# A two-block transformer kernel on one core: the mixer starts with its gated columns, and softmax sums are divided out by products with a diagonal matrix

## The chip, the cores and the metric

The kernel runs on one core of a Trainium2 chip. The metric is device microseconds for one execution. Five queues of instructions matter: PE (TensorE, matrix products; PEld is its weight load), DVE (VectorE), ACT (ScalarE), POOL (GpSimd) and SP, which issues every DMA. Each takes its instructions strictly in the order in which they were written out when the program was built; they wait for each other by semaphores.

## The reference, cut to what matters

The program is a chain of two blocks. The first has two layers, each a mixer, a cross-attention and a gated feed-forward part; the second is a single layer with a recurrent mixer and sixteen experts. Only the mixer of the first block's two layers is touched. It reads 512 tokens of width 1024:

```
proj = x @ w_in + b_in
c_q, c_kv, k_r, u = split(proj)          # 256, 256, 32 and 2 * 512 columns
q  = rms_norm(c_q) @ w_uq                # 8 heads of 64 + 32 columns
kv = rms_norm(c_kv) @ w_ukv              # keys and values of 8 heads
p  = softmax(mask(q @ k.T) * scale)      # by blocks of 128 queries, causal
y_att  = p @ v
a, g = split(u); h = a * sigmoid(g)      # the gated half
y_conv = silu(layer_norm(conv31(h)))     # 31 taps along the tokens
out = concat(y_att, y_conv) @ w_o
```

## The kernel before

Most products are made of three: each float32 operand is split into a rounded high part and a low rest (`fp32r`), and `mm3` (lines 157 to 159) sums high by high, high by low and low by high. `weight` loads a weight (`wr`), rounds it on ACT (`wh`, line 148) and subtracts on DVE or, for every n-th weight, on POOL (`wl`, line 152); `pool_lo` is that n. The few matrices of plain float32 go through `nc.tensor.matmul` directly. `tr` (line 163) transposes 128 by 128 values on PE with the constant `ident`.

The mixer's parts, in the order of the code before: `latent(0)` makes and normalises the query latent, token block by token block (its DVE lines are 463, 183, 469 and 130, its POOL line 185 is the reciprocal root); `queries` projects it to heads and rotates (DVE lines 261 to 266); `gated(0)` makes two of the four 128-column chunks of h (the product with the whole 512 tokens as moving side, then ACT line 487 and DVE line 488); `latent(1)` makes the key and value latent; `gated(2)` makes the other two chunks. Then come key and value weights (line 542), values, and eight heads.

For each head and each of its four query blocks, a score product (line 601, 128 to 512 columns, float32) is reduced to its maximum on DVE (line 603), exponentiated on ACT with the sum on the side (line 606), the sum is inverted on DVE (line 608), the block is scaled by that on ACT (line 609), transposed on PE (line 163) and copied out by DVE (line 613) for the product with the values (line 622). In the code the convolution comes after the heads: chunks 0 and 2 are 31 DVE instructions each (666, 670, copy 671), chunks 1 and 3 are products with one tap on ACT (677) or POOL (679) and a sum on POOL (680), through two buffers `cm`. 

The code's order is not the order of the engines: a scheduler writes each engine's list when the program is built, and fills it with whatever it holds to be ready, earlier code first. So convolution taps are strewn among the other instructions. Line numbers below are those of the code before; in the code after, lines from 103 on stand 3 higher, those from the heads' loop 3 to 5 higher.

Of the kernel before, what the change touches and what calls it, by code (L numbers as in the profile page):

```python
# [10 lines left out]
F32 = mybir.dt.float32  # L11
F32R = mybir.dt.float32r
I32 = mybir.dt.int32
AF = mybir.ActivationFunctionType
# [42 lines left out]
class Builder:  # L57
# [42 lines left out]

    def sm(self, shape=(1,), dt=F32):
        return self.sp.tile([128] + list(shape), dt, name="sm", tag="sm", bufs=20)

    def ring(self, *ids):

        state = [0]

        def bank():
            i = ids[state[0] % len(ids)]
            state[0] += 1  # L110
            return self.pp.tile([128, 512], F32, name=f"q{i}", tag=f"q{i}", bufs=1)

        return bank
# [324 lines left out]
    def mixer(self, l, xT):  # L438
        nc, A = self.nc, self.A
# [15 lines left out]
        def latent(c):  # L455
            c0, n = (0, 256) if c == 0 else (256, 288)
            ring = self.ring(0, 1, 2, 3)
            ps = self.tok_cols(w_in, c0, n, xT, ring, tokens_first=c == 0)
            ss = self.sm([NT])
            ct = [self.s2([2, 256]) for _ in range(2)]  # L460
            for t in range(NT):
                x = ct[t // 2][:, t % 2, :]
                nc.vector.tensor_tensor(out=x, in0=ps[t][:, 0:256], in1=bc[:, c0:c0 + 256], op=OP.add)
                if c == 1:
                    nc.vector.tensor_tensor(out=krt[:, t, 64:96], in0=ps[t][:, 256:288], in1=bk, op=OP.add)
                junk = self.s2([256])
                nc.scalar.activation(junk, x, AF.Square, accum_out=ss[:, t:t + 1])
                r = self.rstd(ss[:, t:t + 1], 1.0 / 256, EPS)
                nc.vector.scalar_tensor_tensor(x, x, r, gn[:, c, :], op0=OP.mult, op1=OP.mult)
                pt = ring()[:, :256].rearrange("p (k t) -> p k t", k=2)  # L470
                for k in range(2):
                    self.tr(pt[:, k, :], x[:, k * 128:(k + 1) * 128])
                dst = (cq, ck)[c]
                s = slice(t * 128, (t + 1) * 128)
                self.split_ps(pt, dst[:, 0, :, s], dst[:, 1, :, s])
# [19 lines left out]
        def queries():  # L495

            ring = self.ring(4, 5, 6)
            for i in range(2):
                nc.scalar.activation(qt[i][:, :, :, 96:100],
                                     self.qm[:, 2 * i:2 * i + 2, None, :].to_broadcast([128, 2, 8, 4]), AF.Copy)  # L500
            for hf in range(2):
                wh, wl = self.weight(A["mla_w_uq"][l][:, hf * 384:(hf + 1) * 384]
                                     .rearrange("(k p) f -> p k f", p=128), [2, 384])
                for t in range(NT):
                    ps = ring()[:, :384]
                    s = slice(t * 128, (t + 1) * 128)
                    for k in range(2):
                        self.mm3(ps, cq[:, 0, k, s], cq[:, 1, k, s], wh[:, k, :], wl[:, k, :], k == 0, k == 1)
                    nc.scalar.activation(qt[t // 2][:, t % 2, 4 * hf:4 * hf + 4, 0:96],
                                         ps.rearrange("p (h d) -> p h d", h=4), AF.Copy, scale=QSCALE)  # L510
            for i in range(2):
                self.rope(qt[i][:, :, :, 64:80], qt[i][:, :, :, 80:96], 2 * i, 2, 8)

        latent(0)
        queries()
        gated(0)
        latent(1)
        gated(2)
        self.pool_lo = 5
        kr = krt.rearrange("p t (h d) -> p t h d", h=1)  # L520
        self.rope(kr[:, :, :, 64:80], kr[:, :, :, 80:96], 0, NT, 1)

# [35 lines left out]
        mm = nc.tensor.matmul  # L558
# [31 lines left out]
        for h in range(HEADS):  # L590
            if h + 1 < HEADS:
                if h % 2 == 1:
                    keys(h + 1)
                query(h + 1)
            kh, q = key(h), qs.pop(h)
            pair = h // 2 % 2
            pts = [(ptas[pair][i], ptbs[pair][:, i]) for i in range(2)]
            for t in range(NT):
                nv = (t + 1) * 128
                ps = sring()  # L600
                mm(ps[:, :nv], q[:100, t * 128:nv], kh[:100, :nv], start=True, stop=True)
                nm = self.sm([1])
                nc.vector.tensor_reduce(nm, ps[:, :nv], axis=AX.X, op=OP.max, negate=True)
                p = self.s2([512])
                sum_ = self.sm([1])
                nc.scalar.activation(p[:, :nv], ps[:, :nv], AF.Exp, bias=nm, accum_out=sum_)
                rc = self.sm([1])
                nc.vector.reciprocal(rc, sum_)
                nc.scalar.activation(p[:, :nv], p[:, :nv], AF.Copy, scale=rc)
                pt = tring().rearrange("p (k t) -> p k t", k=4)  # L610
                for k in range(t + 1):
                    self.tr(pt[:, k, :], p[:, k * 128:(k + 1) * 128])
                nc.vector.tensor_copy(pts[h % 2][t // 2][:, :t + 1, (t % 2) * 128:(t % 2) * 128 + 128], pt[:, :t + 1, :])
            if h % 2:

                ps = cring()
                for i in range(2):
                    n = 2 * i + 2
                    for k in range(n):
                        for j in range(2):  # L620
                            hd = slice((h - 1 + j) * 64, (h + j) * 64)
                            mm(ps[j * 64:j * 64 + 64, i * 256:(i + 1) * 256], vt[:, k, hd], pts[j][i][:, k, :],  # L622
                               start=k == 0, stop=k == n - 1)
                self.split_ps(ps, yT.hi(h // 2), yT.lo(h // 2))
# [218 lines left out]

    def first_block(self):
        A = self.A
        self.phase(t8=11, s2=10, cm=2)
        self.rope_tables()
        xT = self.transposed(self.ring(4, 5, 6, 7))
        for l in range(LAYERS):
            yT = self.mixer(l, xT)  # L850
            self.stage(f"cln{l}")
            gb = self.ln_params(A["ln1_g"][l], A["ln1_b"][l])
            self.out_proj(A["mix_w_o"][l], yT, gb)
            self.stage(f"wo{l}")
            mT, kT = self.memory_keys(l)
            xT = self.transposed(self.ring(4, 5, 6, 7))
            vh, vl = self.memory_values(l, mT)
            self.stage(f"kv{l}")
            self.dump(f"ln1_{l}", self.xt)
            self.stage(f"ln1_{l}")  # L860
            oT = self.cross(l, xT, kT, vh, vl)
            self.stage(f"cross{l}")
            gb2 = self.ln_params(A["ln2_g"][l], A["ln2_b"][l])
            if l + 1 == LAYERS and "ctx_2" in A:
                self.setup2()
            xT, ring = FM(self, 8, 512), self.ring(3, 4)
            self.out_proj(A["xa_w_o"][l], oT, gb2, lambda t: self.tr_tile(self.xt[:, t, :], xT, t, ring=ring))
            self.dump(f"ln2_{l}", self.xt)
            self.stage(f"ln2_{l}")
            self.side = (self.adaln, self.context)[l]() if "ctx_2" in A else None  # L870

            def norm3():
                gb3 = self.ln_params(A["ln3_g"][l], A["ln3_b"][l])
                token = self.token_start() if l + 1 == LAYERS and "ctx_2" in A else lambda t: None

                def finish(t):
                    self.layer_norm(t, gb3)
                    token(t)

                return finish  # L880

            self.ffn(l, xT, norm3, iter(self.TICKS[l] * 64))
            self.dump(f"ln3_{l}", self.xt)
            self.stage(f"ln3_{l}")
            if l + 1 < LAYERS:
                xT = self.transposed(self.ring(4, 5, 6, 7))
# [944 lines left out]
    def second_block(self):  # L1831
        if self.dbg and self.dbg.get("skip1"):
            self.setup2()
            self.phase(t8=11, s2=10, cm=2)
            self.pc = self.ring(3, 7)
            for part in (self.adaln, self.context):
                for _ in part():
                    pass
            self.stage("ctx")
            token = self.token_start()  # L1840
            for t in range(NT):
                token(t)
        cat = self.token_mixer()
        self.stage("cat")
        self.moe(cat)
        self.phase()
# [58 lines left out]
```

## Time and profile before

| what | value |
|---|---|
| median of 3 runs | 2583.95 us (2583.64 to 2584.36) |
| the profiled execution | 2585.66 us, its span 2583.9 us |
| PE busy | 2436.6 us, 94% of the span |
| DVE busy | 1334.9 us, 52% |
| ACT busy | 899.2 us, 35% |
| POOL busy | 624.7 us, 24% |
| mixer of layer 0 up to its first softmax | 0 to 123.1 us |
| its heads | 123.1 to 184.5 us and a little more |
| mixer of layer 1: first softmax, last | 922.1 and 982.9 us |

Busy shares are of the whole span. The mixers hold about 190 us each of it, and their shares are quite different, so the stretches of the mixers have to be read by themselves. A busy PE is modelled: the ends of matrix products overlap, and starts tell more of its pace than durations.

### The profile page before, as it was taken

The numbers are of one execution on the slowest core, as the hardware profiler recorded it, in microseconds if no ns is written. First come the engines' busy times: TensorE is split into PE (matmuls) and PEld (weight loads), VectorE is DVE, ScalarE is ACT, GpSimd is POOL, SyncE is SP. The second block draws the span as 40 slices with busy tenths as digits, with TensorE's granted clock in tenths as the row PEclk, the third lists the DMA queues.
The fourth block names the chain that finished last, engine by engine and source line by source line (L and its number), as shares of the span: only waits on it lengthen the run. The fifth ranks groups of instructions, "written<-read, shape, count | busy, mean of one in ns | idle before, by whom it ended". The sixth has DMA issues, their size and how long they took to land.

```text
span 2583.9 us, 32689 instructions
## 1 busy us (share of the span) xinstructions
PE 2436.6 (94%) x12732; PEld 1809.5 (70%) x12732; DVE 1334.9 (52%) x2197; ACT 899.2 (35%) x1603; POOL 624.7 (24%) x471
## 2 busy tenths in 40 slices
PE   7989999999998979998999999989899699999997
PEld 6747887777776847887888888878788544343432
DVE  4977446754547786646554343565668711111113
ACT  4673442222222574443335342363462211011101
POOL 2862112221113583103221111223415200000000
PEclk9999999999999999999999999999889799999998
DMA  5312422554543311522333222221012479999996
GB/s 156 90 41 74 153 83 62 183 158 152 180 147 102 102 33 66 156 90 82 92 99 91 81 92 72 66 75 52 15 34 83 162 284 409 409 409 409 409 409 254
DMA packets 207510, 395.13 MB, mean 153 GB/s; under 512 B 24080, under 2 KB 115352, under 8 KB 207356
## 3 DMA queue, kind: packets, MB, share of 16 engines
q1 hardware_dynamic: 207356, 393.05, 43.8%
q8 instruction: 100, 1.64, 0.3%
q14 instruction: 54, 0.44, 0.1%
HBM read 390.87 MB, written 2.13 MB: 152 GB/s over the span
## 4 chain that ended last, share of the span: by engine, by line
PE 81%; DVE 12%; ACT 3%; DMA 2%; issue 1%; POOL 1%; SPq 0%; DVEq 0%; POOLq 0%; ACTq 0%
PE q L157 17%; PE q L158 17%; PE q L159 17%; PE q L1754 12%; PE q L163 3%; PE q L1791 2%; DVE q L670 1%; PE q L1729 1%; DVE wl L152 1%; PE q L1181 1%; PE q L1186 1%; PE q L1755 1%; DVE xt L281 1%; PE q L622 1%; DVE s L1157 1%
## 5 line engine op out<-in xcount | busy, mean ns | idle before, releaser
L157 PE MATMUL q<-t,wh 128*128 128x512 f32 (+1 forms) x1320 | 491.4, 373 | 9.5 <-DVE t L130 4.4
L158 PE MATMUL q<-t,wh 128*128 128x512 f32 (+1 forms) x1320 | 491.2, 372 | 1.7 <-DVE t L1482 1.1
L159 PE MATMUL q<-t,wl 128*128 128x512 f32 (+1 forms) x1320 | 488.6, 372 | 0.0
L148 ACT ACTIVATE wh<-wr 128x1024 fp32r<-128x1024 f32 (+3 forms) x280 | 289.1, 1034 | 522.2 <-PE q L159 228.0
L152 DVE TENSOR_TENSOR wl<-wr,wh 128x1024 fp32r<-128x1024 f32 (+3 forms) x206 | 267.4, 1299 | 222.8 <-ACT wh L148 216.4
L157 PE MATMUL q<-wh,t 128*128 128x512 f32 (+4 forms) x964 | 365.2, 384 | 11.7 <-ACT wh L148 4.5
L158 PE MATMUL q<-wl,t 128*128 128x512 f32 (+4 forms) x964 | 362.7, 378 | 2.5 <-POOL wl L152 1.2
L159 PE MATMUL q<-wh,t 128*128 128x512 f32 (+4 forms) x964 | 359.3, 379 | 0.3 <-DVE t L130 0.2
L152 POOL TENSOR_TENSOR wl<-wr,wh 128x1024 fp32r<-128x1024 f32 (+2 forms) x74 | 183.8, 2486 | 638.9 <-ACT wh L148 561.3
L157 PEld LDWEIGHTS q<-t,wh 128*128 128x128 f32 x1320 | 251.3, 191 | 58.6 <-DVE t L130 4.9
L158 PEld LDWEIGHTS q<-t,wh 128*128 128x128 f32 x1320 | 251.7, 191 | 44.2 <-DVE t L1482 1.4
L159 PEld LDWEIGHTS q<-t,wl 128*128 128x128 f32 x1320 | 251.5, 191 | 41.0 <-DVE wl L152 0.4
L185 POOL TENSOR_TENSOR sm<-sm,mhalf 128x1 f32<-128x1 f32 (+3 forms) x75 | 72.6, 970 | 758.7 <-DVE sm L183 757.2
L157 PEld LDWEIGHTS q<-wh,t 128*128 128x128 f32 x964 | 183.8, 191 | 55.1 <-DVE xt L292 6.4
L158 PEld LDWEIGHTS q<-wl,t 128*128 128x128 f32 x964 | 184.3, 191 | 35.2 <-POOL wl L152 1.7
L159 PEld LDWEIGHTS q<-wh,t 128*128 128x128 f32 x964 | 183.2, 191 | 35.9 <-issue 0.9
L680 POOL TENSOR_TENSOR t<-t,cm 128x511 f32<-128x511 f32 (+14 forms) x120 | 147.1, 1226 | 25.6 <-ACT cm L677 20.5
L801 POOL TENSOR_TENSOR t<-cm,t 128x512 fp32r<-128x512 f32 x44 | 70.4, 1600 | 301.3 <-ACT t L800 301.3
L163 PE MATMUL q<-ident,s 128*128 128x128 f32 (+3 forms) x538 | 95.2, 286 | 49.1 <-DVE s L1692 13.2
L163 PEld LDWEIGHTS q<-ident,s 128*128 128x128 f32 (+3 forms) x538 | 63.9, 143 | 107.5 <-issue 29.7
L128 ACT ACTIVATE t<-q 128x512 fp32r<-128x512 f32 (+1 forms) x124 | 63.3, 540 | 106.3 <-PE q L163 59.3
L1764 ACT ACTIVATE s<-q 128x512 f32<-128x512 f32 x16 | 9.6, 597 | 249.1 <-PE q L1755 249.1
(442 smaller groups left out, 4021.4 us busy)
## 6 DMA issues: line engine op xcount, KB each, us to landing
wr<-in_ffn_w_in SPq DMA_DIRECT2D x88, 512.0 KB
t<-in_w_down SPq DMA_DIRECT2D x50, 512.0 KB
wr<-in_w_mod SPq DMA_DIRECT2D x48, 512.0 KB
t<-in_w_up SPq DMA_DIRECT2D x48, 512.0 KB
t<-in_w_gate SPq DMA_DIRECT2D x46, 512.0 KB
wr<-in_ffn_w_down SPq DMA_DIRECT2D x44, 512.0 KB
wr<-in_w_gate SPq DMA_DIRECT2D x33, 512.0 KB
wr<-in_xa_w_kv SPq DMA_DIRECT2D x32, 512.0 KB
```

What stands on the lines that cost most here:

```text
L128: nc.scalar.activation(hi, ps, AF.Copy, scale=1.0 if scale is None else scale)
L148: nc.scalar.activation(hi, raw, AF.Copy)
L152: e.tensor_tensor(out=lo, in0=raw, in1=hi.bitcast(F32), op=OP.subtract)
L157: m(out, ah, bh, start=first, stop=False)
L158: m(out, ah, bl, start=False, stop=False)
L159: m(out, al, bh, start=False, stop=last)
L163: self.nc.tensor.transpose(out, in_, self.ident[:n, :n])
L185: nc.gpsimd.tensor_tensor(out=r, in0=v, in1=self.mhalf[:, :n], op=OP.pow)
L680: nc.gpsimd.tensor_tensor(out=acc[:, i, d:], in0=acc[:, i, d:], in1=m, op=OP.add)
L801: nc.gpsimd.tensor_tensor(out=hl[:, j + i, :], in0=sg, in1=hh[:, j + i, :].bitcast(F32), op=OP.subtract)
L1754: mm(ps[lo_, :], x, raw[:, c0], start=first, stop=last)
L1791: mm(ps, cts[e][h, ts], ys[e][h, s, :], start=i + s == 0, stop=i + s == len(es))
```

## The change

It has two parts that touch instructions. The mixer calls its parts in the order `gated(0)`, `latent(0)`, `gated(2)`, `queries`, `latent(1)`, with `pool_lo` going back to 5 ahead of `latent(1)`. In the heads the block of exponentials is no longer scaled on ACT: ACT scales the identity by the inverted sums instead (`dg`, always 128 by 128), and PE multiplies the unscaled block with it, which transposes and divides at once. To hold the tiles the pools get one more buffer of `t8` and of `s2`, four of `dg`, and a DMA scratch area is made smaller; no transfer of this program is issued from POOL.

```
-        latent(0)
-        queries()
         gated(0)
+        latent(0)
+        gated(2)
+        queries()
+        self.pool_lo = 5
         latent(1)
-        gated(2)
-        self.pool_lo = 5
...
                 rc = self.sm([1])
                 nc.vector.reciprocal(rc, sum_)
-                nc.scalar.activation(p[:, :nv], p[:, :nv], AF.Copy, scale=rc)
+                dg = self.dg()
+                nc.scalar.activation(dg, self.ident, AF.Copy, scale=rc)
                 pt = tring().rearrange("p (k t) -> p k t", k=4)
                 for k in range(t + 1):
-                    self.tr(pt[:, k, :], p[:, k * 128:(k + 1) * 128])
+                    mm(pt[:, k, :], p[:, k * 128:(k + 1) * 128], dg, start=True, stop=True)
...
+    def dg(self):
+        return self.sp.tile([128, 128], F32, name="dg", tag="dgm", bufs=4)
...
-        self.phase(t8=11, s2=10, cm=2)
+        self.phase(t8=12, s2=11, cm=2)
...
-    nc = bacc.Bacc("TRN2", target_bir_lowering=False, num_devices=1)
+    nc = bacc.Bacc("TRN2", target_bir_lowering=False, num_devices=1, dynamic_dma_scratch_size=1024)
```

How the scheduler's lists move with it is seen at three places. The first is DVE's list in layer 0 around the first maximum of the heads (`TENSOR_REDUCE`, line 603 before, 606 after). Before, the taps of the second convolution chunk (line 670, the bank q_1633) stand between the first softmax steps:

```order
133 L152 TENSOR_TENSOR wl<-wr,wh 128x1024
134 L670 SCALAR_TENSOR_TENSOR q_1633<-t_198,cvec,q_1633 128x505
135 L575 COPY n_915<-q_984 64x512
136 L529 COPY n_916<-q_910 36x1024
137 L670 SCALAR_TENSOR_TENSOR q_1633<-t_198,cvec,q_1633 128x504
138 L603 TENSOR_REDUCE sm<-q_1007 128x1
139 L670 SCALAR_TENSOR_TENSOR q_1633<-t_198,cvec,q_1633 128x503
140 L608 RECIPROCAL sm<-sm 128x1
141 L603 TENSOR_REDUCE sm<-q_1020 128x1
```

After, the last tap (482 columns, line 675 is 670 before) and its copy stand ahead of the first maximum:

```order
153 L675 SCALAR_TENSOR_TENSOR q_1665<-t_198,cvec,q_1665 128x483
154 L532 COPY n_916<-q_910 36x1024
155 L675 SCALAR_TENSOR_TENSOR t_199<-t_198,cvec,q_1665 128x482
156 L676 COPY t_199<-q_1665 128x30
157 L133 TENSOR_TENSOR t_197<-q_883,t_197 128x2x128
158 L133 TENSOR_TENSOR t_197<-q_897,t_197 128x2x128
159 L578 COPY n_915<-q_984 64x512
160 L155 TENSOR_TENSOR wl<-wr,wh 128x1024
161 L578 COPY n_916<-q_1069 64x512
162 L606 TENSOR_REDUCE sm<-q_1007 128x1
```

Of the 60 taps of line 670 in a layer, 38 stood ahead of the first maximum before in layer 0 and 39 in layer 1, and all 60 do now. ACT's list changes likewise: all its tap products stand ahead of its first exponential.

The second place is PE's list at the program's start, where x is transposed (line 163, 166 after) and the first products follow. Before, products of `latent(0)` on the first token block (256 columns) stand among the transposes:

```order
5 L163 MATMUL q_116<-ident,xt 128x128 x4
6 L157 MATMUL q_203<-wh,t_112 128x256
7 L163 MATMUL q_158<-ident,xt 128x128 x4
8 L157 MATMUL q_202<-wh,t_112 128x256
9 L158 MATMUL q_202<-wl,t_112 128x256
10 L158 MATMUL q_203<-wl,t_112 128x256
```

After, all transposes stand ahead of the first product of `gated(0)`, whose moving side is all 512 tokens:

```order
5 L166 MATMUL q_116<-ident,xt 128x128 x4
6 L166 MATMUL q_158<-ident,xt 128x128 x4
7 L166 MATMUL q_144<-ident,xt 128x128 x4
8 L166 MATMUL q_151<-ident,xt 128x128 x4
9 L166 MATMUL q_165<-ident,xt 128x128 x4
10 L160 MATMUL q_276<-t_112,wh 128x512
```

Layer 1 begins in the same two ways, with products of `latent(0)` among the transposes of the layer's input before and none after.

The third place is POOL's list where `latent(1)` is normalised (the reciprocal root on `mhalf`, line 185 before, 188 after). Before, these stand after the sixth sum (line 680) of the first POOL chunk:

```order
20 L680 TENSOR_TENSOR t_199<-t_199,cm 128x508
21 L680 TENSOR_TENSOR t_199<-t_199,cm 128x507
22 L152 TENSOR_TENSOR wl<-wr,wh 128x1024
23 L680 TENSOR_TENSOR t_199<-t_199,cm 128x506
24 L185 TENSOR_TENSOR sm<-sm,mhalf 128x1 x2
```

After, that chunk is summed to its end (482 columns) and the next one is begun before the first of them:

```order
54 L684 TENSOR_SCALAR cm<-t_198,cvec 128x482
55 L685 TENSOR_TENSOR t_199<-t_199,cm 128x482
56 L685 TENSOR_TENSOR t_199<-t_199,cm 128x511
57 L685 TENSOR_TENSOR t_199<-t_199,cm 128x510
58 L188 TENSOR_TENSOR sm<-sm,mhalf 128x1
```

Beyond the mixers the lists of all engines are the same but for a few neighbours that change places.

## Rows read from the trace of the kernel before

**Rows 1.** The page: busy time, share of the span, instructions.
```profile
PE 2436.6 (94%) x12732; PEld 1809.5 (70%) x12732; DVE 1334.9 (52%) x2197; ACT 899.2 (35%) x1603; POOL 624.7 (24%) x471
```
**Rows 2.** Windows: length; busy us of PE, PEld, DVE, ACT, POOL; PE clock; DMA.
```profile
67.00:123.00 56.00, 50.84 (x263) 42.88 (x262) 53.89 (x81) 36.79 (x58) 48.83 (x47) 0.95 0.33 95
123.00:184.00 61.00, 52.17 (x249) 28.62 (x247) 47.07 (x121) 49.69 (x120) 48.65 (x50) 0.96 0.14 44
...
866.00:922.00 56.00, 50.92 (x265) 42.73 (x265) 53.92 (x81) 36.58 (x58) 47.13 (x45) 0.97 0.33 95
```
**Rows 3.** Timeline of DVE: start us, us, operation; splits, first taps, first maxima.
```profile
21.22 2.47 DVE L130 TENSOR_TENSOR t<-q,t 128x512 fp32r<-128x512 f32 x4
...
36.00 1.22 DVE L152 TENSOR_TENSOR wl<-wr,wh 128x1024 fp32r<-128x1024 f32 x1
...
67.04 0.81 DVE L666 TENSOR_SCALAR q<-t,cvec 128x512 f32<-128x512 f32 x1
...
123.13 0.29 DVE L603 TENSOR_REDUCE sm<-q 128x1 f32<-128x128 f32 x1
...
866.16 0.81 DVE L666 TENSOR_SCALAR q<-t,cvec 128x512 f32<-128x512 f32 x1
...
922.07 0.29 DVE L603 TENSOR_REDUCE sm<-q 128x1 f32<-128x128 f32 x1
```
**Rows 4.** DVE's groups from 67 to 123 us: busy us, mean ns, idle before.
```profile
L670 DVE SCALAR_TENSOR_TENSOR q<-t,cvec,q 128x511 f32<-128x511 f32 (+28 forms) x37 | 27.2, 736 | 0.6
L152 DVE TENSOR_TENSOR wl<-wr,wh 128x1024 fp32r<-128x1024 f32 (+1 forms) x6 | 9.5, 1576 | 0.6 <-ACT wh L148 0.6
...
L469 DVE SCALAR_TENSOR_TENSOR s<-s,sm,s 128x256 f32<-128x256 f32 x4 | 3.6, 921 | 0.0
...
L463 DVE TENSOR_TENSOR s<-q,s 128x256 f32<-128x256 f32 x4 | 1.7, 416 | 0.3 <-PE q L159 0.3
```
**Rows 5.** Timeline of PE: first gated products of both layers, last transposes of layer 1's input.
```profile
48.38 0.40 PE L157 MATMUL q<-t,wh 128*128 128x512 f32 x1
...
831.55 1.04 PE L163 MATMUL q<-ident,xt 128*128 128x128 f32 x8
...
847.50 0.39 PE L157 MATMUL q<-t,wh 128*128 128x512 f32 x1
```
**Rows 6.** Timeline of PE: first score product of heads 0, 3, 4 and 7, layer 0.
```profile
121.20 1.20 PE L601 MATMUL q<-n,s 100*128 100x128 f32 x3 [1.29 <-DVE n L575]
...
149.75 0.38 PE L601 MATMUL q<-n,s 100*128 100x128 f32 x2
...
156.95 0.38 PE L601 MATMUL q<-n,s 100*128 100x128 f32 x1
...
179.75 0.39 PE L601 MATMUL q<-n,s 100*128 100x128 f32 x2
```
**Rows 7.** Timeline of PE: transposes and float32 products in turn, second block.
```profile
1861.15 1.04 PE L163 MATMUL q<-ident,wr 128*128 128x128 f32 x8
1862.03 1.06 PE L1181 MATMUL q<-wr,s 128*128 128x128 f32 x8
1862.92 0.60 PE L163 MATMUL q<-ident,wr 128*128 128x128 f32 x4
```
**Rows 8.** ACT's groups from 123 to 184 us, all forms of a line together.
```profile
L609 ACT ACTIVATE s<-s,sm 128x128 f32<-128x128 f32 (+3 forms) x30 | 16.5, 552 | 7.1 <-DVE sm L608 7.0
...
L677 ACT ACTIVATE cm<-t,cvec 128x511 f32<-128x511 f32 (+15 forms) x16 | 11.1, 707 | 0.4 <-POOL t L680 0.3
```
**Rows 9.** ACT's groups of the same stretch, forms apart: the smallest scaling.
```profile
L609 ACT ACTIVATE s<-s,sm 128x128 f32<-128x128 f32 x8 | 3.2, 399 | 2.6 <-DVE sm L608 2.6
```
**Rows 10.** Waits of the weight loads from 123 to 184 us: total us, times, longest.
```profile
PEld q L163 <- ACT s L609: 11.5, 18, 1.4
PEld q L601 <- ACT s L606: 6.5, 13, 1.8
```
**Rows 11.** POOL's groups from 74 to 128 us.
```profile
L680 POOL TENSOR_TENSOR t<-t,cm 128x511 f32<-128x511 f32 (+29 forms) x30 | 39.3, 1311 | 2.8 <-ACT cm L677 1.5
...
L185 POOL TENSOR_TENSOR sm<-sm,mhalf 128x1 f32<-128x1 f32 x4 | 3.5, 890 | 0.0
```
**Rows 12.** Timeline of POOL: the first sums.
```profile
74.35 2.46 POOL L680 TENSOR_TENSOR t<-t,cm 128x511 f32<-128x511 f32 x2 [0.41 <-ACT cm L677]
```
**Rows 13.** Windows, layer 0, columns as in rows 2.
```profile
30.00:40.00 10.00, 4.56 (x18) 3.44 (x17) 3.34 (x10) 4.39 (x13) 3.79 (x3) 0.79 0.37 106
```

More of the change, by code (lines that the diff above doesn't have):

```diff
@@ L512, in queries @@
                 self.rope(qt[i][:, :, :, 64:80], qt[i][:, :, :, 80:96], 2 * i, 2, 8)
+        gated(0)
         latent(0)
+        gated(2)
         queries()
-        gated(0)
+        self.pool_lo = 5
         latent(1)
-        gated(2)
-        self.pool_lo = 5
         kr = krt.rearrange("p t (h d) -> p t h d", h=1)
@@ L1833, in second_block @@
             self.setup2()
-            self.phase(t8=11, s2=10, cm=2)
+            self.phase(t8=12, s2=11, cm=2)
             self.pc = self.ring(3, 7)
```

## The prediction, on record before the run

> **What bounds the kernel now.** I read the page's busy shares first, then windows over the two touched mixers, then the groups and waits inside them. The page makes PE look like the bound, 94% busy [rows 1], but that is a mean over stages, and most of the program isn't touched. The windows say otherwise for the mixers. From the first convolution tap to the first maximum of the heads, 67 to 123 us in layer 0 and 866 to 922 us in layer 1, DVE is busy 53.89 and 53.92 of 56 us, and PE 50.8 and 50.9 by a model that counts overlapping ends twice over [rows 2]. So DVE bounds this stretch, in both layers alike, and the reader should see there a fixed list of work on one engine that has to run down before the heads can begin. The timeline gives its ends: first tap at 67.04, first maximum at 123.13 us, and 866.16 and 922.07 us in layer 1 [rows 3]. Inside it, 37 taps take 27.2 us, 736 ns each [rows 4].
>
> In the heads no engine is full: from 123 to 184 us DVE has 47.1, ACT 49.7 and PE 52.2 of 61 us [rows 2]. The first score products of heads 0, 3, 4 and 7 stand at 121.20, 149.75, 156.95 and 179.75 us [rows 6]: 9.5 us a head for the first three, with taps between their steps, then 7.2, then 7.6 for the last three. PE waits 11.5 us for the scaled block and 6.5 us for the exponentials [rows 10], some 2.2 us in each of the eight heads. That is a chain through PE, DVE and ACT, more than a load.
>
> What stands behind a mixer waits for its end, so I take a shift in a mixer as a shift of the program's end.
>
> **The start.** The new list has all transposes of the mixer's input ahead of the first gated product. In layer 0 the four splits of one group start at 21.22 and take 2.47 us [rows 3], so the inputs of that product are complete between 21.2 and 23.7 us; before, it started at 48.38 us, and in layer 1 at 847.50 us [rows 5]. From there to the first tap (24 triple products for each of the four banks, weights, the gate) it took 18.66 us in both layers (67.04 less 48.38, 866.16 less 847.50). Kept at that, the first tap comes at 40 to 42.4 us in layer 0; I take 41. In layer 1 the last transposes start at 831.55 and take 1.04 us [rows 5]; with one split of 0.62 us (a quarter of 2.47) the first gated product starts at 832 to 833, and the first tap is at 851. One risk: from 30 to 40 us PE was granted 0.79 of full clock [rows 13], between its two levels, after a start with many idle gaps. The new order has such gaps again, in layer 1 too. If the gated products meet 0.79 for 10 us they lose 2.1 us of full speed, so each first tap could come up to 3 us later.
>
> **DVE's list up to the first maximum.** It keeps the 56.1 us of before (123.13 less 67.04; 55.9 in layer 1) and gains what moved in front of the first maximum or behind the first tap:
> - 22 taps in layer 0 (60 less 38), 21 in layer 1, of 0.736 us [rows 4]: 16.2 and 15.5 us.
> - The query latent's normalisation, four token blocks, which before was done ahead of the first tap: 0.416 us (line 463) and 0.921 us (line 469) [rows 4], one more of 128x256 taken like line 463, and one single column for which I estimate 0.15: 1.9 each, 7.6 us.
> - Twelve instructions of the heads' rotation, shorter or as long as line 463: 5.0 us.
> - Weight remainders of 1920 columns, at 1576 ns for 1024 [rows 4]: 3.0 us.
> - One copy of keys, taken like a split: 0.6 us.
>
> That is 32.4 us. Successive instructions overlap a little at their seams, so I take 6% off, which is a choice, and have 30.5: the stretch is 87 us. Its bounds are 84, if remainders cost 1.22 us, as the one at 36.00 us does [rows 3], and the overlap is larger, and 89 without any overlap. The first maximum then comes at 41 + 87 = 128 us in layer 0, **5 us later** than 123.13, and at 851 + 87 = 938 us in layer 1, **16 us later** than 922.07. The layers differ because in layer 1 the query latent used to run token block by token block while the input's last blocks were still being made ready, and the gated products can't: their moving side is all 512 tokens.
>
> **The other lists in that stretch.** POOL's first sum came 7.3 us after the first tap, at 74.35 us [rows 12]; a sum takes 1311 ns and 30 of them with their waits fill 74 to 128 us [rows 11]. The new list finishes that whole chunk ahead of the key latent's reciprocal root (0.89 us each, four of them [rows 11]). So the root comes at 41 + 7.3 + 54 = 102 us or later in layer 0, and the keys, the last thing that the heads need, come behind it: values, copies and splits on DVE, whose list holds them near its end anyway. ACT's tap products now all stand ahead of its first exponential, and wait for POOL to free the two buffers `cm`; 16 of them still stood in 123 to 184 us, at 707 ns [rows 8], and 16 × 1.31 = 21 us of sums pace them. 102 plus the second chunk's ACT share ends at about 125, beside DVE's 128. I cost this wait at nothing since DVE hides it by 3 us; without that cover it costs what it exceeds (rival B').
>
> The remainders of line 152 show that DVE is slower beside POOL: 1.22 us at 36.00 us, ahead of the first sum [rows 3], 1576 ns on average beside the sums [rows 4], 0.36 more. About 18 instructions with two inputs in SBUF come into the stretch (remainders, rotations, line 469); the rotations I took without such a share. If each paid 0.36 more than taken, that would be 6.5 us a layer (rival B); I take nothing, since line 469's mean is already one from beside POOL.
>
> The Trainium skill, "SBUF — State Buffer", section "SBUF: two separate sides", says that VectorE and GpSimd share a port pair under an exclusive lock, so that a VectorE instruction with two SBUF inputs and a GpSimd instruction that reads SBUF block each other for their whole length. The 0.36 us points that way but is smaller than a whole instruction. By the rule, with half a sum (0.65 us) of waiting for each of the 18, the sum would be 12 us a layer higher, and the median 2617.
>
> **The heads.** Per head ten transposes of `p` become ten plain products. In the second block eight transposes span 0.88 us (1861.15 to 1862.03) and the four float32 products behind them, 8 records, 0.89 [rows 7]: 0.110 and 0.222 us each, so 1.1 us more of PE a head, 9 a layer. ACT's scaling was 552 ns on average [rows 8] and is now always of the smallest size, 399 [rows 9]: 0.6 us less a head. With all taps gone from DVE and ACT the heads start from the pace of the last three, 7.6 us. PE's 1.1 is hidden if it fits into the 2.2 us of waits, and costs 1.1 if not; I take half, 0.55, since PE, DVE and ACT all have gaps but work in turn. ACT's 0.6 lies on the path, since PE waits for just that result. So 7.6 + 0.55 − 0.6 = 7.5 us a head. Seven heads take 52.5 in place of 58.55 us: **6 us less** a layer, in layer 1 too by its like windows. Bounds: 6.0 (all waits gone and ACT's part too, 7.6 + 1.1 − 2.2 − 0.6) and 8.7 (7.6 + 1.1).
>
> The buffers of `t8`, `s2` and `dg` and the smaller scratch cost no instruction: nothing, unless one of them lets a third head be in flight, which belongs to rival A.
>
> **The sum.** 5 + 16 − 6 − 6 = +9 us. The profiled execution took 2585.66 us, 1.7 over the median shown; so 2594.7 for such a one, and a median of **2593**. A measurement of this kernel can tell about 0.2%, 5.2 us, from no change.
>
> **The rivals.**
> - **A, faster: the heads run freely.** Once no tap stands between their steps, PE finds another head ready whenever it waits, and a head costs 6.0 to 6.4 us. At 6.2 seven heads take 43.4 us, 15 less a layer: 21 − 30 = −9, a median of 2575; at 6.0, −12, and with a DVE stretch of 84 us in both layers 2566. It decides where a head costs under 6.5 us (21 less 2 × 13.1 is −5). For it: all PE's waits are for ACT [rows 10], which gets shorter. Against: undisturbed heads with DVE at rest for much of the time still took 7.6 [rows 6].
> - **A', no change:** heads of 6.5 to 7.2 us give −5 to +5, about 2584.
> - **B, slower still: DVE is held up beside POOL.** 18 instructions of 0.36 us more, 6.5 a layer, a median of 2606. For it: the remainders' two durations. Against: the stretch of before, DVE and POOL both nearly full (53.9 and 48.8 of 56 us [rows 2]), gave the means that I use. This is what the section of the Trainium skill named above speaks for.
> - **B', POOL paces the first exponential.** If its first chunk takes longer than 54 us, ACT's last tap product comes behind DVE's list; it decides from about 3 us over, and at 5 to 8 us a layer the median is 2603 to 2609. Against: DVE was the fuller one.
> - **C, the division moved buys nothing:** PE pays its 1.1 in full, 8.7 us a head, 60.9 for seven; each layer gains 2 instead of losing 6, the end is +26 and the median 2610. Against it stand the 2.2 us of waits.
>
> **How the numbers follow.** The forecast's own case has 0.40 (first maxima at +5 and +16 within 4 us, heads 7.2 to 7.9), between 2589 and 2600. A 0.22, A' 0.20, B 0.09, B' 0.05, C 0.04. The tenth below reaches into A, 2568; the tenth above into B and B', 2608. Faster is A, 0.22; within 0.2% A' and the forecast's lower edge, 0.22; the rest, 0.56, slower.
>
> **What would show it.** A first tap at 40 to 43 and 850 to 854 us; DVE over 95% busy from there to the first maximum, which stands at 126 to 131 and 935 to 941 us; product spacing of 0.22 us where the transposes of `p` were; heads 7.2 to 7.9 us apart, evenly. The prediction is wrong if DVE's stretch is far from 87 us, if ACT waits for POOL at the first exponential (B'), or if heads stand closer than 6.5 us (A).

## The result and the profile after

| | before | after |
|---|---|---|
| median | 2584.15 us (2583.64 to 2588.9, 4 runs) | 2617.56 us (2616.68 to 2621.38, 4 runs) |
| ratio, 95% interval | | 1.0131 (1.0115 to 1.0147) |
| span of the profiled execution | 2583.9 us | 2614.6 us |

The changed kernel is slower by 33 us. 2593 was forecast, with 2608 as the end of the range: the sign was right, and the size was nearly four times too small.

The timeline of DVE in the changed kernel (start us, us, operation; in square brackets the idle time before it and what ended it), layer 0 and then layer 1. These rows answer to [rows 3]:

```profile
42.65 0.81 DVE L671 TENSOR_SCALAR q<-t,cvec 128x512 f32<-128x512 f32 x1
...
126.82 0.18 DVE L676 COPY t<-q 128x30 f32<-128x30 f32 x1
126.92 0.75 DVE L133 TENSOR_TENSOR t<-q,t 128x256 fp32r<-128x256 f32 x2
133.19 0.68 DVE L578 COPY n<-q 64x512 f32<-64x512 f32 x1 [5.53 <-PE q L162]
133.80 1.21 DVE L155 TENSOR_TENSOR wl<-wr,wh 128x1024 fp32r<-128x1024 f32 x1
134.93 0.68 DVE L578 COPY n<-q 64x512 f32<-64x512 f32 x1
136.60 0.29 DVE L606 TENSOR_REDUCE sm<-q 128x1 f32<-128x128 f32 x1 [0.99 <-PE q L604]
...
861.86 0.81 DVE L671 TENSOR_SCALAR q<-t,cvec 128x512 f32<-128x512 f32 x1
...
947.17 0.18 DVE L676 COPY t<-q 128x30 f32<-128x30 f32 x1
949.22 0.68 DVE L578 COPY n<-q 64x512 f32<-64x512 f32 x1 [1.87 <-PE q L162]
...
952.61 0.29 DVE L606 TENSOR_REDUCE sm<-q 128x1 f32<-128x128 f32 x1 [0.98 <-PE q L604]
```

The first tap came at 42.65 us, and the taps ran down to 127 us, close to the forecast (41, and 128 us for the whole list). But the first maximum isn't the end of that list. Behind the last tap stand the last splits of the key latent at 126.92, then 5.53 us in which DVE waits for PE to make values and the first keys from them, then the copies and the scores: 136.60 us. The windows over both stretches of both layers (length; busy us of PE, PEld, DVE, ACT, POOL; PE clock; DMA), which answer to [rows 2]:

```profile
42.65:127.67 85.02, 65.85 (x382) 58.39 (x381) 83.84 (x131) 49.23 (x89) 73.57 (x70) 0.90 0.28 80
127.67:136.60 8.93, 8.03 (x33) 6.32 (x33) 2.42 (x4) 5.71 (x10) 4.44 (x4) 0.81 0.04 3
861.86:947.30 85.44, 67.73 (x397) 60.45 (x396) 83.82 (x131) 49.22 (x88) 71.17 (x67) 0.90 0.26 75
947.30:952.60 5.30, 4.41 (x25) 3.53 (x24) 2.46 (x4) 4.60 (x9) 3.38 (x4) 1.00 0.07 5
```

DVE is full for 85 us and then has 2.4 us of work in 8.9. In the kernel before, taps were left over for such gaps, and the first maximum stood right behind one. What PE did meanwhile is in its timeline:

```profile
100.62 0.29 PE L162 MATMUL q<-wh,t 128*128 128x288 f32 x1
114.44 0.66 PE L166 MATMUL q<-ident,s 128*128 128x128 f32 x2 [13.52 <-DVE s L264]
117.78 0.66 PE L166 MATMUL q<-ident,s 128*128 128x128 f32 x2 [2.68 <-DVE s L268]
118.16 0.79 PE L160 MATMUL q<-wh,t 128*128 128x512 f32 x1
118.75 0.63 PE L161 MATMUL q<-wl,t 128*128 128x512 f32 x1
119.18 0.63 PE L162 MATMUL q<-wh,t 128*128 128x512 f32 x1
...
122.57 0.39 PE L162 MATMUL q<-wh,t 128*128 128x512 f32 x1
122.80 0.40 PE L160 MATMUL q<-wh,t 128*128 128x512 f32 x1
```

At 100.62 us PE starts the last product of `latent(1)` and then has nothing left, since `gated(2)` is already done. It stands still for 13.5 us until DVE has normalised the first token block (line 472, done at 114.29 us; the wait's row names line 264, the DVE instruction that ended last before it), and for 15.0 us in layer 1. DVE is busy through all of it, and the granted clock was 0.64 on average:

```profile
100.80:114.40 13.60, 0.12 (x1) 0.00 (x0) 13.60 (x27) 5.92 (x14) 11.03 (x13) 0.64 0.28 87
```

The products that follow start 0.43 us apart (118.75 to 119.18) where the ones at 122.57 and 122.80 us start 0.23 apart.

PE's timeline, first score products of heads 0 and 7, the first pair in layer 0 and the second in layer 1, which answers to [rows 6]:

```profile
136.07 0.92 PE L604 MATMUL q<-n,s 100*128 100x128 f32 x4 [0.90 <-ACT s L588]
...
189.56 0.39 PE L604 MATMUL q<-n,s 100*128 100x128 f32 x2
...
952.09 0.92 PE L604 MATMUL q<-n,s 100*128 100x128 f32 x4 [0.89 <-ACT s L588]
...
1005.54 0.39 PE L604 MATMUL q<-n,s 100*128 100x128 f32 x2
```

Seven heads take 53.5 us in both layers, 7.64 each on average. An even pace was forecast; in both layers the seven steps are 7.0, 6.5, 10.2, 6.0, 9.0, 6.0 and 8.8 us.

**Where the time went.** For each instruction that both lists share I took its start after less its start before (the lag). Its median is 10.6 us in the stretch behind layer 0's mixer, 7.8 just ahead of layer 1's, 28.2 behind that, 33.1 from 1300 us on, and 31.1 at the end. So layer 0's mixer costs 10.6 us, layer 1's 20.4, and 5 us come in one step near 1250 us, where the lists are the same but for a few neighbours. There the clock is lower for a while, by the windows of the changed kernel (columns as above) and, in the second fence, the corresponding ones of the kernel before:

```profile
1270.00:1280.00 10.00, 8.44 (x43) 7.13 (x41) 6.27 (x9) 5.61 (x12) 3.90 (x4) 0.76 0.28 89
1280.00:1290.00 10.00, 10.00 (x37) 8.00 (x37) 5.06 (x9) 1.36 (x2) 2.17 (x1) 0.72 0.18 52
```

```profile
1240.00:1250.00 10.00, 9.56 (x66) 8.29 (x65) 7.04 (x11) 5.62 (x12) 3.39 (x4) 1.00 0.32 111
1250.00:1260.00 10.00, 9.73 (x44) 7.43 (x43) 7.33 (x13) 2.20 (x4) 3.60 (x3) 1.00 0.37 110
```

The rest are −2.8 and −2.0 us. The first comes at about 800 us, where the kernel before had the lower clock (0.74 from 790 to 810 us, against 0.91 from 800 to 820 in the changed kernel); the second comes in several steps between 1680 and 2000 us, and its cause isn't shown. All this is read from one traced execution of each kernel.

### The profile page after: what moved, and what is told of

It is laid out like the page before. It is cut to its first block, busy times and chain, and to the rows that moved or that the text cites. A ratio compares the mean times of both kernels' runs of the same rounds, so it can differ in the third digit from the quotient of the medians.

```text
span 2614.6 us, 33020 instructions
## 1 busy us (share of the span) xinstructions
PE 2451.1 (94%) x12892; PEld 1833.8 (70%) x12892; DVE 1345.1 (51%) x2198; ACT 893.6 (34%) x1603; POOL 625.2 (24%) x470
## 4 chain that ended last, share of the span: by engine, by line
PE 80%; DVE 12%; ACT 3%; issue 2%; POOL 2%; DMA 1%; SPq 0%; DVEq 0%; POOLq 0%; ACTq 0%
PE q L160 17%; PE q L161 16%; PE q L162 16%; PE q L1759 12%; PE q L166 3%; PE q L1796 2%; DVE q L675 1%; DVE wl L155 1%; PE q L617 1%; PE q L1186 1%; PE q L1734 1%; PE q L1191 1%; PE q L604 1%; PE q L627 1%; PE q L1760 1%
## 5 line engine op out<-in xcount | busy, mean ns | idle before, releaser
L155 DVE TENSOR_TENSOR wl<-wr,wh 128x1024 fp32r<-128x1024 f32 (+2 forms) x207 | 266.4, 1288 | 220.7 <-ACT wh L151 214.0
L155 POOL TENSOR_TENSOR wl<-wr,wh 128x1024 fp32r<-128x1024 f32 (+3 forms) x73 | 183.1, 2510 | 630.9 <-ACT wh L151 566.2
L685 POOL TENSOR_TENSOR t<-t,cm 128x511 f32<-128x511 f32 (+14 forms) x120 | 149.1, 1243 | 23.1 <-ACT cm L682 17.6
L166 PE MATMUL q<-ident,s 128*128 128x128 f32 (+3 forms) x378 | 66.2, 292 | 55.8 <-DVE sm L186 15.0
L166 PEld LDWEIGHTS q<-ident,s 128*128 128x128 f32 (+3 forms) x378 | 46.5, 148 | 93.4 <-issue 57.7
```

The costliest lines, as they stand in the source:

```text
L155: e.tensor_tensor(out=lo, in0=raw, in1=hi.bitcast(F32), op=OP.subtract)
L166: self.nc.tensor.transpose(out, in_, self.ident[:n, :n])
L685: nc.gpsimd.tensor_tensor(out=acc[:, i, d:], in0=acc[:, i, d:], in1=m, op=OP.add)
```

## The experiments

Theory 1 from this: the order costs everything, by DVE's long list and by the bare chain behind it. The rivals: the diagonal products cost a good part; the start of the mixer does; POOL does. In the table a layer's first maximum is given against the kernel before; for layer 1 the lag just ahead of its mixer is taken off. "Heads" is the first score of head 7 less that of head 0, in layers 0 and 1. Both are read from the traced execution; a ratio is to runs of the kernel before that were made beside it.

| kernel | median us | ratio (95%) | first maximum, layers 0, 1 | heads us |
|---|---|---|---|---|
| before | | | 0, 0 | 58.5, 57.9 |
| after | 2617.56 | 1.0131 (1.0115 to 1.0147) | +13.5, +22.7 | 53.5, 53.5 |
| new order, ACT scales | 2605.69 | 1.0075 (1.0060 to 1.0090) | +13.0, +21.4 | 51.0, 48.3 |
| old order, diagonal products | 2584.84 | 0.9995 (0.9986 to 1.0005) | −2.0, −0.8 | 57.9, 56.0 |
| only gated(0) ahead | 2602.00 | 1.0065 (1.0048 to 1.0082) | +1.7, +15.2 | 57.2, 56.8 |
| only gated(2) ahead | 2603.68 | 1.0075 (1.0055 to 1.0094) | +8.5, +7.9 | 58.4, 55.2 |
| after, second tap chunk late | 2600.81 | 1.0056 (1.0041 to 1.0071) | +3.2, +18.3 | 55.6, 55.0 |
| after, 22 taps left out | 2602.05 | 1.0064 (1.0050 to 1.0078) | +4.5, +16.5 | 53.4, 53.7 |
| after, no POOL taps | 2588.69 | 1.0014 (1.0005 to 1.0023) | −0.4, +13.1 | 52.5, 52.5 |
| gated(0) ahead, taps late | 2598.03 | 1.0053 (1.0037 to 1.0070) | +1.8, +15.6 | 56.1, 56.6 |
| old order, diagonal, taps late | 2577.46 | 0.9969 (0.9957 to 0.9981) | −5.0, −4.1 | 57.6, 57.4 |
| old order, ACT scales, taps late | 2577.70 | 0.9970 (0.9960 to 0.9980) | −5.4, −2.6 | 61.2, 59.8 |

What the stretches between the mixers take differs by some us from kernel to kernel (the lag just ahead of layer 1's mixer goes from −5.8 to +7.8), so a few us of a total aren't to be explained from the mixers.

### The two parts apart

The new order with the old division, and its difference from the changed kernel:

```
-                dg = self.dg()
-                nc.scalar.activation(dg, self.ident, AF.Copy, scale=rc)
+                nc.scalar.activation(p[:, :nv], p[:, :nv], AF.Copy, scale=rc)
...
-                    mm(pt[:, k, :], p[:, k * 128:(k + 1) * 128], dg, start=True, stop=True)
+                    self.tr(pt[:, k, :], p[:, k * 128:(k + 1) * 128])
```

> The changed kernel with the division put back to ACT's scaling and PE's transposes; the new order and buffers stay. Theory 1 (the order costs everything: DVE's 60 taps stand ahead of the first maximum, and behind them the chain from the last key split to the first maximum is bare): the same first maxima as the changed kernel, 136.6 and 952.6 us, heads within 0.5 us of 7.6, so 2617 us, 2611 to 2622. Theory 2 (the diagonal products cost a good part: 1.1 us of PE a head, 9 a layer): heads near 6.7 us, 2600 to 2606.

2605.69 us: theory 2's range, 12 us under the changed kernel. The old order with the new division:

```
-        gated(0)
         latent(0)
-        gated(2)
         queries()
-        self.pool_lo = 5
+        gated(0)
         latent(1)
+        gated(2)
+        self.pool_lo = 5
```

> The kernel before with the diagonal products and the new buffers, in the old order of the mixer's parts. Theory 1: first maxima as before (123.1 and 922.1 us), heads within 0.5 us of before, 2584 us, 2579 to 2589. Theory 2: heads about 1 us slower, 2595 to 2602.

2584.84 us, no difference, where theory 2 wanted 11 us or more. This kernel also has the new buffers and the smaller scratch, so they cost nothing either. Theory 2 was met by the first kernel and theory 1 by the second: neither holds alone. The order costs about 20 us by itself, and the diagonal products cost something only in the new order, where no tap stands between the steps of the heads. The windows over seven heads of layer 1, first with the old division in the new order, then (second fence) the changed kernel:

```profile
950.00:998.60 48.60, 44.70 (x232) 25.18 (x232) 28.47 (x85) 41.56 (x102) 32.70 (x34) 1.00 0.18 65
```

```profile
952.10:1005.50 53.40, 51.32 (x290) 35.12 (x291) 28.39 (x85) 37.89 (x102) 32.98 (x34) 0.97 0.18 60
```

With bare heads the old division takes 6.9 us a head and the new one 7.64; PE is then busy 51.3 of 53.4 us, so its longer products come through, while ACT's 3.7 us of relief (41.56 to 37.89) don't show in the heads' pace. This is 2.5 us in layer 0 and 5.2 in layer 1; the 5 us near 1250 us, which this kernel doesn't have (its lag is 19.2 ahead of it and 19.5 behind), are most of the rest of the 12.

### Which part of the order

Only `gated(0)` ahead, against the changed kernel:

```
         gated(0)
         latent(0)
-        gated(2)
         queries()
-        self.pool_lo = 5
         latent(1)
+        gated(2)
+        self.pool_lo = 5
```

> The changed kernel, but with only the first gated part moved ahead: gated(0), latent(0), queries, latent(1), gated(2). 41 taps stand ahead of the first maximum in each layer (60 in the changed kernel, 38 and 39 before). Theory 1: DVE's list up to the first maximum is 14 us shorter (19 taps of 0.74) and the chain to it is filled with taps, heads some 4 to 6 us a layer slower; 2595 to 2602. Rival (the cost is the gated product's wait for all 512 tokens and the clock behind it): the first maxima stay within 4 us of the changed kernel's and the time is 2612 to 2625.

And only `gated(2)` ahead of `latent(1)`:

```
-        gated(0)
         latent(0)
-        gated(2)
         queries()
+        gated(0)
+        gated(2)
         self.pool_lo = 5
         latent(1)
```

> The kernel before with the diagonal products, and only gated(2) moved ahead of latent(1): latent(0), queries, gated(0), gated(2), latent(1). 51 and 49 taps stand ahead of the first maximum (38 and 39 before); the first tap comes as before. Theory 1 (what costs is that nothing is left for PE behind the key latent, and DVE's filler is used up): PE stands still for 10 us or more ahead of the keys in each layer, first maxima 8 to 14 us later than before, heads 3 to 5 us faster; 2592 to 2604. Rival (the cost is the gated product at the mixer's start): within 4 us of 2584.

Both lie at the upper edge of theory 1's ranges (2602.0 and 2603.7), and the table shows that they cost in different places. `gated(2)` ahead of `latent(1)` delays the first maximum by 8 us in both layers; the heads, expected 3 to 5 us faster, got 2.8 us faster in layer 1 and no faster in layer 0. PE's timeline of this kernel shows the same standstill as above, shorter (8.4 us in two pieces, and 8.0 in layer 1, where 10 or more were expected):

```profile
110.54 0.66 PE L166 MATMUL q<-ident,s 128*128 128x128 f32 x2 [5.59 <-DVE s L472]
114.01 0.66 PE L166 MATMUL q<-ident,s 128*128 128x128 f32 x2 [2.81 <-DVE s L472]
```

`gated(0)` ahead costs 1.7 us in layer 0 and 15.2 in layer 1. Together that is 10.2 and 23.1 us, against 13.5 and 22.7 in the changed kernel.

### How much DVE's list decides

The changed kernel with the second chunk's taps held back; the bank that they sum in first takes one column of the first head's keys, which is then overwritten:

```
             w = lambda j: cv[:, i, j:j + 1]
+            if i == 2:
+                nc.vector.tensor_copy(sums[0:64, 0:1], after_[0:64, 0:1])
             nc.vector.tensor_scalar(sums, hs[:, i, :], w(30), w(31), op0=OP.mult, op1=OP.add)
...
-        self.conv(hs, acc, cv)
+        self.conv(hs, acc, cv, key(0))
```

> The changed kernel with the second DVE chunk's taps held back until the first head's keys are copied (a one-column copy that its bank has to wait for): 30 taps stand ahead of the first maximum instead of 60, 30 among the heads. Theory 1: the first maximum comes 20 to 28 us earlier in each layer (30 taps of 0.74 less, and some of the bare chain), the heads take 8 to 11 us a layer more; 2585 to 2597. Rival (POOL sets it: the key latent's reciprocal root stands behind the whole first POOL chunk, done at 106 us in layer 0): the first maximum comes at most 8 us earlier and the slower heads eat it up; 2612 to 2622.

And with 22 taps left out:

```
-            for j in range(29, -1, -1):
+            for j in (range(29, -1, -1) if i == 0 else range(7, -1, -1)):
                 d = 30 - j
                 out = sums[:, d:] if j else acc[:, i, d:]
```

> The changed kernel with 22 of the second DVE chunk's 30 taps left out (that part of the convolution isn't computed): 38 taps stand ahead of the first maximum as before the change, none among the heads. Theory 1 (DVE's list, then a chain from the last key split): the list is 16 us shorter, but the kernel with late taps showed a second limit about 10 us below the changed kernel's first maximum, so first maxima 9 to 12 us earlier in each layer and 2592 to 2600. If the taps were only filler and something else set the first maximum: 2612 or more.

The first missed its range (2600.8 against 2585 to 2597), and the second's was set by it and holds in layer 0, while its time is 2 us over. Taking 16 or 22 us out of DVE's list brings the first maximum forward by 9 to 10 us in layer 0 and by 4 to 6 in layer 1, no further. DVE's timeline of the kernel with 22 taps less shows what stands there then:

```profile
105.44 0.41 DVE L466 TENSOR_TENSOR s<-q,s 128x256 f32<-128x256 f32 x1
...
118.53 0.76 DVE L133 TENSOR_TENSOR t<-q,t 128x256 fp32r<-128x256 f32 x2 [0.45 <-ACT t L131]
124.27 0.68 DVE L578 COPY n<-q 64x512 f32<-64x512 f32 x1 [4.99 <-PE q L162]
...
127.67 0.29 DVE L606 TENSOR_REDUCE sm<-q 128x1 f32<-128x128 f32 x1 [0.99 <-PE q L604]
```

From DVE's first work on the key latent (105.44) to the first maximum it is 22 us, mostly a chain through DVE, POOL, ACT and PE, and no shorter list helps it: it begins when PE has made that latent and DVE has gone through the rotations ahead of it, and with `gated(2)` ahead that latent is PE's last work.

The same hold where only `gated(0)` is ahead:

> The kernel with only gated(0) moved ahead, diagonal products, and the second DVE chunk's taps held back behind the first keys: 30 taps ahead instead of 41. If what gated(0) costs at the front is DVE's load ahead of the keys, first maxima come 6 to 9 us earlier than in the kernel without the hold (124.8 and 937.2 us), heads 2 to 5 us slower: 2590 to 2598. If it is the start of the mixer (the product with all 512 tokens waits for the last transposes, and PE runs at the lower clock behind): no earlier than 121 and 933 us, 2600 or more.

The first maxima stayed at 124.9 and 937.8 us, so in this order the taps didn't set them at all; the time, 2598.0, lies at the end of the first case's range and under the second's. That leaves the mixer's start for what `gated(0)` costs in layer 1. Two windows of the changed kernel, and (second fence) two of the kernel before, up to its first gated product:

```profile
830.00:840.00 10.00, 3.60 (x17) 2.59 (x16) 8.99 (x11) 1.79 (x3) 2.78 (x2) 0.58 0.40 106
840.00:850.00 10.00, 10.00 (x38) 7.67 (x37) 1.69 (x3) 1.20 (x2) 0.00 (x0) 0.74 0.01 2
```

```profile
822.20:832.20 10.00, 8.58 (x71) 7.96 (x71) 9.51 (x15) 2.66 (x8) 2.33 (x2) 1.00 0.36 97
832.20:847.50 15.30, 14.14 (x88) 12.46 (x87) 9.09 (x23) 9.42 (x23) 4.77 (x6) 1.00 0.17 49
```

Before, PE worked on the query latent while DVE made the last tokens ready, and then on the queries, all at full clock. After, it stands still for most of ten us, and starts the gated products at a granted clock of 0.74; the query latent has to be paid for later, on PE as much as on DVE. The windows from just ahead of layer 1's mixer to its first score product show what that does to PE, in the kernel before, with only `gated(0)` ahead, and in the changed kernel (one fence each):

```profile
815.00:920.15 105.15, 97.17 (x535) 83.00 (x535) 84.10 (x136) 55.06 (x96) 59.27 (x54) 0.98 0.34 92
```

```profile
815.00:935.96 120.96, 101.88 (x534) 86.92 (x534) 94.36 (x139) 55.15 (x97) 72.50 (x65) 0.92 0.30 82
```

```profile
822.80:952.09 129.29, 101.45 (x541) 86.71 (x541) 106.08 (x161) 63.60 (x108) 81.82 (x74) 0.88 0.26 73
```

PE has much the same instructions to run each time (534 to 541, counting transposes). Before it idled for 8.0 us of that stretch; with `gated(0)` ahead it idles for 19.1 and takes 4.7 us longer over the products, at a lower mean clock, which is the 15.8 us by which the first score is late. So PE was nearly full here before, and time that it loses at the start isn't made up. That the whole of it comes from the start isn't shown: two of its waits, of 2.7 and 2.4 us, come later (at 872 and 907 us).

### What POOL costs DVE

The changed kernel without POOL's chunks:

```
-        for i in self.CONV_POOL:
+        for i in ():
             for j in range(29, -1, -1):
```

> The changed kernel without the POOL chunks' products and sums (half the convolution isn't computed, ACT's tap products fall away too). DVE's list keeps all 60 taps ahead of the first maximum. Port theory (DVE's instructions with two inputs in SBUF wait for POOL): in layer 0 their 12 us above the shortest of their kind vanish, first tap to last tap takes 73 to 76 us instead of 84, first maxima come 9 to 13 us earlier in each layer; 2590 to 2600. Rival (the excess is not POOL's): the stretch stays within 3 us and the time at 2608 to 2618.

DVE's groups (line, operation, count; busy us, mean ns; idle before) over the list with the taps, from 42.6 to 127.8 us in the changed kernel, and (second fence) from 43 to 122 us without POOL's taps:

```profile
L675 DVE SCALAR_TENSOR_TENSOR q<-t,cvec,q 128x511 f32<-128x511 f32 (+28 forms) x58 | 42.6, 735 | 1.0
L155 DVE TENSOR_TENSOR wl<-wr,wh 128x1024 fp32r<-128x1024 f32 (+2 forms) x7 | 10.9, 1553 | 0.0
L472 DVE SCALAR_TENSOR_TENSOR s<-s,sm,s 128x256 f32<-128x256 f32 x8 | 7.7, 970 | 0.0
...
L267 DVE TENSOR_TENSOR t<-t,cos 128x256 f32<-128x256 f32 x2 | 2.1, 1036 | 0.0
```

```profile
L675 DVE SCALAR_TENSOR_TENSOR q<-t,cvec,q 128x511 f32<-128x511 f32 (+28 forms) x58 | 42.7, 736 | 1.0
L155 DVE TENSOR_TENSOR wl<-wr,wh 128x1024 fp32r<-128x1024 f32 (+2 forms) x8 | 9.1, 1142 | 0.9 <-ACT wh L151 0.9
L472 DVE SCALAR_TENSOR_TENSOR s<-s,sm,s 128x256 f32<-128x256 f32 x8 | 3.8, 477 | 0.5 <-POOL sm L188 0.5
...
L267 DVE TENSOR_TENSOR t<-t,cos 128x256 f32<-128x256 f32 x2 | 0.8, 417 | 0.0
```

The normalisations, with both inputs in SBUF, halve from 970 to 477 ns, a rotation goes from 1036 to 417, and the taps, one of whose inputs is a PSUM bank, stay at 735. The stretch from the first tap to the end of the last falls from 84.2 to 74.7 us, as the port theory wanted, and the first maximum comes 13.9 us earlier in layer 0. This is what "SBUF — State Buffer", section "SBUF: two separate sides", of the Trainium skill leads one to look for; the runs agree with it on which instructions are held up. Without POOL's sums ACT and POOL also give the key latent's root at once, so not all of the 13.9 us are the port's. In layer 1 13.1 us of the 22.7 remain, which fits the start. The time, 2588.7 us, lies just under the port theory's range; ACT's and POOL's work on the taps is gone from the heads too.

That POOL sums a whole chunk ahead of the key latent's reciprocal root (line 188) didn't delay that root in the changed kernel. POOL stood ready and waited for DVE, in layer 0 and in layer 1:

```profile
112.40 0.56 POOL L188 TENSOR_TENSOR sm<-sm,mhalf 128x1 f32<-128x1 f32 x1 [1.23 <-DVE sm L186]
...
931.96 0.55 POOL L188 TENSOR_TENSOR sm<-sm,mhalf 128x1 f32<-128x1 f32 x1 [1.23 <-DVE sm L186]
```

### A version that beats both

The old order with the late taps, with the diagonal products and then without:

> The kernel before (old order) with the diagonal products and with the second DVE chunk's taps held back behind the first head's keys: 30 taps ahead of the first maximum instead of 38, 30 among the heads. Theory 1: DVE bounds the stretch ahead, so the first maximum comes 4 to 6 us earlier per layer, and 8 more taps in the heads give 2 to 5 of it back; 2576 to 2584. Rival (PE or POOL is as full there): no earlier maximum, slower heads, 2588 to 2595.

> The old order with the second DVE chunk's taps held back (as in the version with the diagonal products that gained 0.3%), but with ACT's scaling and PE's transposes. If the late taps alone make the gain: 2575 to 2580, first maxima at 118 and 914 us. If the diagonal products are needed for it (ACT is spared 0.15 us a block while taps stand among the heads): heads 1 to 3 us slower a layer, 2580 to 2585.

Both gain 0.3% on the kernel before (0.9969 and 0.9970). With 30 taps ahead instead of 38 the first maxima came at 118.1 and 117.7 us in layer 0, 5 us earlier, about the eight taps' 5.9 us. In the profiled executions the diagonal products save 3.6 and 2.4 us of heads here, where ACT has tap products between, but the two times don't differ, so what they are worth in this kernel stays open within some 3 us.

## Why the prediction was too low

- **The step that failed** is the one from DVE's list to the first maximum. The text saw that the keys come behind the key latent's root, and counted them at nothing, as "values, copies and splits on DVE, whose list holds them near its end anyway"; the first maximum was put at the first tap plus the list. The chain of values, keys and scores begins only with that list's last entries (the split at 126.92 us) and lies behind it, in series: 8.9 us in layer 0 and 5.3 in layer 1 before the first maximum. The order listing had shown it, since all 60 taps stood ahead and none was left as filler; I counted the taps as work and not as the cover that they had been. Measured with the start, the first maximum was late by 13.5 and 22.7 us instead of 5 and 16.
- **The start.** The first tap was forecast for 41 and 851 us and came at 42.7 and, with the lag of 7.8 us taken off, 854.1. In layer 1 the 3 us are the price that the text gave for a lower clock and did not put into the sum: PE was granted 0.86 from 838.90 to 861.86 us. In layer 0 it had 1.00 from 24.00 to 42.65 us; there ACT's gate (line 490) began only at 41.15 us, right behind the load of an activation table that took 1.28 us.
- **DVE's list.** 87 us were forecast, 85.0 and 85.4 were measured. The parts were off against each other: the twelve rotations of 256 columns took 9.7 us instead of 5.0 beside POOL, since they were priced like line 463, one of whose inputs is a PSUM bank (414 ns beside POOL and 416 without its taps), while the rotations read SBUF twice. The weight remainders added 0.8 us instead of 3.0, and more overlap at the seams and less idle time made up for the rest. Rival B named the mechanism, and the runs bear it out, but the list as a whole held.
- **A number that came true by luck.** The prediction also works out a median of 2617, by half a sum of waiting for each of 18 instructions. The measured 2617.56 is no support for it: that sum makes DVE's list 12 us a layer longer than 87, and the list was 2 us shorter.
- **The +16 of layer 1** was worked out along DVE alone, as first tap plus list. With 22 taps less on DVE 16.5 us remained, and with 30 late taps and `gated(2)` back behind 15.6: PE's lost overlap at the start holds the first maximum nearly as late, and DVE's list was only the longer of two limits some 6 to 7 us apart. That fits how little shortening the list gave back. The text had set PE's 50.8 and 50.9 of 56 us aside as counted twice where products overlap; but the windows never give an engine more than their length (10.00 of 10.00 us over 88 products), so PE had been nearly as full as DVE.
- **The heads.** 7.5 us were forecast, 7.64 came, 5 us less for seven heads. The spacing of 0.22 us for the new products came too (three in 0.67 us from 189.78), but the sum was wrong in both parts: without taps the old division would have given 7.3 and 6.9 us, so the taps' leaving brought more, and PE's longer products took 2.5 to 5 us of it back, where the forecast had them and ACT's relief cancel. Rival C put that at 7.7 us, PE paying in full; layer 1 came nearer to it than to the forecast, layer 0 did not.
- **Rival B'** did not decide: POOL waited for DVE at the root, and ACT's last tap product ahead of the first exponential ended at 137.1 us, 1.9 us ahead of it, with a copy and a table load of 1.28 us between.
- **Not foreseen:** the 5 us near 1250 us, in a stretch that the change doesn't touch.

Together: forecast −1 and +10 us for the two mixers; measured +10.6 and +20.4, which is 22 us more. The chain behind the list is 14.2 of these, the later first taps 4.7, the heads 2.5; the shorter list takes 3.6 off. Another 2.8 us come from measuring by the first maximum: before, the first score product stood 1.9 us ahead of it and now 0.5, so the heads' start is 1.4 us later a layer than the first maximum tells. And 0.75 us a layer come behind the last head's first score. The lag at the end (31.1) exceeds the forecast's 9 by the same 22; the 5 us and the two shifts the other way cancel.

## What to carry to other kernels

Filler work is worth something where it stands: before moving it ahead of a dependent chain, ask what the engines will do while that chain runs, and count the chain from the last entry of the full list on, not beside it, and see how full the second engine is. In these runs it was better to have the part with the longest chain behind its result first, and the independent products after it as cover. A saving found in a mixed stretch (ACT's 0.15 us a block) can turn into a cost when the mix goes, since the engine that had room is then the full one.

## What was not expected of the hardware

That DVE's slowdown beside POOL goes so strictly by operands: 58 taps with one input in a PSUM bank took 735 ns beside POOL's sums and 736 without them, while normalisations of 256 columns with both inputs in SBUF took 970 and 477. And that times shift by several us in stretches whose lists are nearly equal: the lag just ahead of layer 1's mixer, after the same 600 us of instructions, differed from the lag behind layer 0's by up to about 4 us. In the changed kernel, and near 1250 us, such a shift goes with granted clocks of 0.72 to 0.91 in one trace or the other; for the other kernels this isn't shown.
